# Two-layer hybrid encoder on one core: another rule for the order of the engines' streams, two means placed later, and the first weight's transfer behind x's first square

## The chip, the cores and the metric

The kernel runs on one core of a Trainium2 chip. The metric is the device time of one execution in microseconds (us), the median of several. The engines of the core work beside one another, each through its own list of instructions in order: TensorE (PE, matmuls), VectorE (DVE), ScalarE (ACT), GpSimd (POOL) and SyncE (SP), which here issues most of the transfers (DMAs). Semaphores make an instruction wait for those of other engines on which it depends.

## The reference

The input is x with 512 positions and 1024 channels, and 256 memory tokens. Each of two layers mixes positions by three attention branches, then channels by a gated MLP:

```
mem_n = rms_norm(mem, mem_norm_g)
for l in range(DEPTH):
    h = rms_norm(x, g_pre_mix[l])
    proj = h @ w_in[l]
    # q, k, v of branch A (2-D neighbourhood attention), of branch B
    # (dilated windows), q of branch M (attention into mem_n @ w_mem_kv[l]), gates
    merged = gates_A * (o_a @ w_br_a[l]) + gates_B * (o_b @ w_br_b[l]) + gates_M * (o_m @ w_br_m[l])
    x = x + rms_norm(merged @ w_out[l], g_post_mix[l])
    h = rms_norm(x, g_pre_ffn[l])
    u = depthwise_conv_centred(h @ w_up[l], conv_w[l], conv_b[l])
    a, b = split(u)
    x = x + rms_norm((gelu(a) * b) @ w_down[l], g_post_ffn[l])
```

rms_norm divides by the root of the mean square over the 1024 channels and multiplies by a gain.

## The kernel before

Channels lie on the partitions: x is eight tiles (KD = 8) of 128 channels by 512 positions, worked on in two halves of 256 positions (`HALVES`). Every matmul operand in float32 is split into a high and a low part of the type fp32r, and one product is three matmuls: high by high, high by low, low by high (`mm3`). The high part is a cast on ACT, the low part a subtraction on DVE or POOL (`split`).

Weights come in pieces of 128 columns, 512 KB. `weights` issues the transfer on SP's queue into a buffer `wraw` (three of them), then splits it, into `whi` and `wlo` (two buffers each) or into tiles `m`. SP issues in its own order, and a transfer waits there until its buffer is free; what stands behind it waits too.

A norm is spread over the engines. ACT squares x, DVE adds the squares, PE sums over the partitions with a matmul by the constant column `mean` (`pt<-mean,y` or `pt<-mean,acc`), ACT takes the root, DVE the reciprocal, PE spreads it over the partitions with two transposes (`pt<-ident,st`), and DVE and ACT make the normed and split `h`. `rstd_job` holds these steps; the functions whose names end in `_job` call it. `pre_norm_job` makes h at the start, for each half of x; `mem_norm_job` does it for the memory tokens; `raw_end_job` is the norm of x's second half at the passage from layer 0 to layer 1.

The order of PE's instructions is set in the code: the class `Woven` keeps a clock that each matmul advances by an assumed cost, and jobs are generators that `yield` a delay; when the clock has passed it, their next instructions are put between the matmuls. `spawn` takes a delay, too: `SD1` is that of `pre_norm_job` for x's second half. Every matmul is chained to the one before it, so this order is fixed. The order on DVE, ACT, POOL and SP is chosen by the framework's scheduler (`TileContext`), from the dependences, the code's order and a simulation of when each instruction could run. The start transfers x's first half in four parts, then the weights of the first group (two pieces, then x's second half, then the vectors, then four pieces of which the buffers allow one at once), and the mask and two tables for the attention. Near 60 us PE makes keys and values from the memory tokens in four products (`mm_704`, `mm_745`, `mm_786`, `mm_819`), with the `mm` pool of three PSUM banks; the results are taken out of the bank by halves by a cast on ACT (`m_729`, `m_770`) and a subtraction on DVE (`m_730`, `m_771`).

Of the kernel before, what the change touches and what calls it, by code (L numbers as in the profile page):

```python
# [9 lines left out]
AF = mybir.ActivationFunctionType  # L10
# [15 lines left out]
HALVES = (slice(0, 256), slice(256, 512))  # L26
# [9 lines left out]
LAT_QK, LAT_SM, LAT_T, LAT_V, LAT_T2 = 1.0, 4.5, 1.5, 2.0, 0.6  # L36
STEP_A, STEP_B, STEP_M = 9.0, 9.0, 5.5
SQG, LOG, GEN, KVE = {0: (), 1: ()}, {0: (), 1: ()}, 'GGVGVG', 'VVGG'
SD1 = 4.0
MARGIN = 0.3  # L40
SB = True
TAILG = (0, 2, 4, 6)
# [77 lines left out]
def tile_hybrid_encoder(ctx, tc, xT, memT, memg, vecs, rpb, w_in, w_kv, w_bra, w_brb, w_brm,  # L120
                        w_out, w_up, w_down, c_ident, c_mask, c_tab0, c_tab1, out):
    nc = tc.nc
# [10 lines left out]
    ps_t = ctx.enter_context(tc.tile_pool(name="ps_t", bufs=2, space=bass.MemoryType.PSUM))  # L133
    ps_o = ctx.enter_context(tc.tile_pool(name="ps_o", bufs=1, space=bass.MemoryType.PSUM))

    uid, last_copy, last_act, crit, last_lo = [0], [None], [None], [None], {}
    wv = Woven(tc)

    def nm(s):
        uid[0] += 1  # L140
        return f"{s}_{uid[0]}"
# [8 lines left out]
    def ktile(dt=F32R, shape=(128, 512)):  # L150
        return tp.tile(list(shape), dt, tag="ka", name=nm("ka"), bufs=12)

    def ytile(shape=(128, 512)):
        return tp.tile(list(shape), F32, tag="y", name=nm("y"), bufs=8)
# [23 lines left out]
    ACT, V = Counted(nc.scalar, wv, 0.1, 0.8e-3), Counted(nc.vector, wv, 0.065, 1.05e-3)  # L178
# [10 lines left out]
    def xh(k, half):  # L189
        return xs[:, half.start // 256, k, :]  # L190
# [23 lines left out]
    tab1 = const.tile([128, 2, 256], F32, name="tab1")  # L214


    def behind(ins, other):

        if other is not None and ins is not other:
            tc.add_manual_dep(ins, other.name, ORDER, reason="issue order")  # L220

    def split(src, hi, lo, eng=None):
        last_copy[0] = ACT.copy(hi, src).ins
        last_lo[eng or V] = (eng or V).tensor_sub(lo, src, f32(hi)).ins

    def weights(src, K, C, slot=None, eng=None, after=None):

        raw = wp.tile([128, K, C], F32, tag="wraw", name=nm("wraw"))
        nc.sync.dma_start(out=raw, in_=src)
        if slot is None:  # L230
            hi = wp.tile([128, K, C], F32R, tag="whi", name=nm("whi"), bufs=2)
            lo = wp.tile([128, K, C], F32R, tag="wlo", name=nm("wlo"), bufs=2)
            split(raw, hi, lo, eng)
            behind(last_copy[0], after)
            return [(hi[:, k, :], lo[:, k, :]) for k in range(K)]
        n = 512 // C
        w = []
        for k in range(0, K, n):
            c = min(n, K - k)
            hi, lo = slot(F32R, (128, c, C)), slot(F32R, (128, c, C))  # L240
            split(raw[:, k:k + c, :], hi, lo, eng)
            w += [(hi[:, i, :], lo[:, i, :]) for i in range(c)]
        return w
# [69 lines left out]
    def sumsq_add(acc, src, first, slot=None, eng=None):  # L313
        if first:
            ACT.activation(acc, src, AF.Square)
        else:
            n = acc.shape[-1]
            sq = slot((128, 256)) if slot else small("sq2", 4) if n == 256 else small("sq", 1, (128, 512))
            ACT.activation(sq, src, AF.Square)
            (eng or V).tensor_add(acc, acc, sq)  # L320
# [4 lines left out]
    def rstd_job(accs, n, box):  # L325

        nb = n // 128
        bank = tbank((128, n + nb))
        pr, pt = bank[:, 0:n], bank[:, n:n + nb]
        for i, a in enumerate(accs):  # L330
            for b in range(nb):
                mm(pt[:, b:b + 1], a[:, 128 * b:128 * b + 128], mean, i == 0 and b == 0,
                   i == len(accs) - 1 and b == nb - 1, 0.11)
        rs = smalls(nb)
        crit[0] = ACT.activation(rs, pt, AF.Sqrt, bias=eps, scale=1.0).ins
        V.reciprocal(rs, rs)
        yield 0.8
        for b in range(nb):
            one = rs[:, b:b + 1]
            spread = bass.AP(one.tensor, one.offset, [list(one.ap[0]), [0, 128]])  # L340
            wv.pe(nc.tensor.transpose(pr[:, 128 * b:128 * b + 128], spread, ident), 0.11)
        box.append(pr)

    def normed(src, g, rs, hi, lo, eng=None):
        h32 = small("h32", 3)
        V.scalar_tensor_tensor(out=h32, in0=src, scalar=g, in1=rs, op0=ALU.mult, op1=ALU.mult)
        split(h32, hi, lo, eng)

    def raw_split(l, goff, k, src, hi, lo):

        g = vec[:, l, goff + k:goff + k + 1]
        ACT.activation(hi, src, AF.Copy, scale=g)
        V.scalar_tensor_tensor(out=lo, in0=src, scalar=g, in1=f32(hi), op0=ALU.mult, op1=ALU.subtract)

    def rtile():
        return tp.tile([128, 512], F32, tag="R", name=nm("R"), bufs=1)
# [6 lines left out]
    def pre_norm_job(l, goff, acc, hs, i):  # L363
        half, box = HALVES[i], []
        yield from rstd_job(acc if isinstance(acc, list) else [acc[:, half]], 256, box)
        for k in range(KD):
            g = g0[:, k:k + 1] if l == 0 and goff == V_PRE else vec[:, l, goff + k:goff + k + 1]
            normed(xh(k, half), g, box[0], hs[k][0][:, half], hs[k][1][:, half],
                   G if k in LOG[l > 0 and goff == V_PRE] else V)
        crit[0] = last_copy[0]  # L370
        yield 1.2
        wv.give(f"h{l}.{goff}.{i}")
# [44 lines left out]
    def raw_end_job(l, goff, og, acc, acc2, nxt, lat):  # L417


        half, box = HALVES[1], []  # L420
        hs, raw, R = nxt
        yield lat
        raw.extend((t[:, 0, :], t[:, 1, :]) for t in [ktile(F32R, (128, 2, 256)) for _ in range(KD)])
        yield from rstd_job([acc[:, half]], 256, box)
        for k in range(KD):
            V.tensor_mul(og[k][:, half], og[k][:, half], box[0])
            V.tensor_add(xh(k, half), xh(k, half), og[k][:, half])
            raw_split(l + 1, V_PRE, k, xh(k, half), *raw[k])
            if k == 0:
                yield 0.6  # L430
            wv.give(f"raw{k}")
            yield 1.05
        for k in range(KD):
            sumsq_add(acc2[:, half], xh(k, half), k == 0)
        yield 3.5
        box = []
        yield from rstd_job([acc2[:, half]], 256, box)
        ACT.copy(R[:, half], box[0])
        wv.give("R")
        for k in range(KD):  # L440
            normed(xh(k, half), vec[:, l + 1, V_PRE + k:V_PRE + k + 1], box[0], hs[k][0][:, half], hs[k][1][:, half])
        crit[0] = last_copy[0]
        yield 1.2
        wv.give(f"h{l + 1}.{V_PRE}.1")
# [33 lines left out]
    def mem_kv(l, hm, km, vm, pre=()):  # L478
        wv.need(f"mem{l}")
        for m in range(4):  # L480
            w = pre[m] if pre else weights(w_kv[l, m], KD, 128)
            ps = mmbank((128, N_MEM))
            linear(ps, w, hm, slice(0, N_MEM))
            if m < 2:
                t, u = big(F32R, (128, 2, N_MEM)), big(F32R, (128, 2, N_MEM))
                twice_split(ps, (t[:, 0, :], t[:, 1, :]), (u[:, 0, :], u[:, 1, :]), None, MDUP)
                km.append((t, u))
            else:
                vT = big(F32, (128, 256))
                ACT.copy(vT, ps)  # L490
                wv.spawn(mem_v_job(l, vT, vm))


    def group_weights(srcs, engs):
        return [weights(s, KD, 128, big, e) for s, e in zip(srcs, engs)]
# [19 lines left out]
    def proj(l, m, hs, after=None):  # L515
        w = weights(w_in[l, m], KD, 128, after=after)
        ps = mmbank()
        linear(ps, w, hs)
        return ps
# [344 lines left out]
    def first_squares(half):  # L864
        sqs = [ytile((128, 256)) for _ in range(KD)]
        for k in range(KD):
            ACT.activation(sqs[k], xh(k, half), AF.Square)
            if k % 2:
                V.tensor_add(sqs[k], sqs[k], sqs[k - 1])
            if k in (3, 5) and half != HALVES[0]:  # L870
                V.tensor_add(sqs[k], sqs[k], sqs[k - 2])
        return sqs[1::2] if half == HALVES[0] else sqs[5::2]
# [10 lines left out]
    idle(2)  # L883
    hs = h_tiles()
    wv.spawn(pre_norm_job(0, V_PRE, first_squares(HALVES[0]), hs, 0))
    gw = group_weights([w_in[0, m] for m in FIRST[:2]], (V, V))
    load_x(HALVES[1])
    nc.sync.dma_start(out=vec, in_=vecs)
    wv.need(f"h0.{V_PRE}.0")
    with tc.issue_after(last_copy[0]):  # L890
        sqs = first_squares(HALVES[1])
    wv.spawn(pre_norm_job(0, V_PRE, sqs, hs, 1), SD1)
    gw += group_weights([w_in[0, m] for m in FIRST[2:]], (V, G, V, G))
# [6 lines left out]
    for l in range(depth):  # L900
# [99 lines left out]
        else:  # L1000
            hm, km, vm = [], [], []
            wv.spawn(mem_norm_job(l + 1, hm, htile), 20.0)
            pre, R, raw, box = [], rtile(), [], []
# [119 lines left out]
```

## Time and profile before

| what | value |
|---|---|
| median of 3 runs | 1555.45 us (1555.26 to 1555.7) |
| profiled execution | 1552.91 us |
| its span (first to last instruction) | 1550.9 us |
| mean granted clock of TensorE | 0.995 |
| instructions | 20677 |
| PE, share of the span | 98% |
| weight loads on PE | 84% |
| DVE | 61% |
| ACT | 48% |
| POOL | 10% |
| moved by DMA | 144.91 MB, mean 93 GB/s |

A row of the timeline has the start in us from the start of the span, the duration, the engine, the line of the kernel, the operation, its output and inputs by their names without numbers, and the shapes. "x4" says that four such instructions stand in a row, with the duration from the start of the first to the end of the last. In brackets stands the idle time of the engine ahead of it, and what ended it. L114 is the line of a helper through which ACT's and DVE's operations go, L246 that of the matmuls, L257 and L341 of transposes, L224 of the split, L229 of the weights' transfers. A row of the windows has the window, its length, the busy time and count of an engine, the granted clock (PEclk), the share of the DMA engines and GB/s.

### The profile page before, as it was taken

Reading aid. Unit: us, or ns where it says so; the run is one execution under the profiler, and the core shown is the slowest. Engines: PE = TensorE matmul, PEld = TensorE weight load, DVE = VectorE, ACT = ScalarE, POOL = GpSimd, SP = SyncE. Lnnn points to the kernel's source line nnn. Section 1 sums busy time; section 2 is a strip of 40 time slices with the busy share of each in tenths; the row PEclk is TensorE's granted clock in tenths of the full one; section 3 lists DMA queues with packets and bytes.
Section 4 is the critical chain, followed back from the end, with each engine's and each line's share of the span. In section 5 each row is a group of like instructions: output and inputs, shape, how many; then the busy total and the mean of one; then the engine's idle time right before and its main releaser. Section 6 shows DMA issues by size and latency. Waiting matters only on the chain.

```text
span 1550.9 us, 20677 instructions
## 1 busy us (share of the span) xinstructions
PE 1522.6 (98%) x7970; PEld 1300.1 (84%) x7970; DVE 948.8 (61%) x1684; ACT 739.7 (48%) x1288; POOL 148.6 (10%) x216
## 2 busy tenths in 40 slices
PE   8999999999999999999989999999999999999997
PEld 7988878888988888888888888888889888888887
DVE  6685666335777777743397856753456977776233
ACT  6465575235544444533355556742354544444231
POOL 3340000210000000010154300002100000000000
PEclk9999999999999999999999999999999999999998
DMA  7221113234112332333431221132350223233331
GB/s 246 91 90 61 61 57 98 93 95 157 61 55 96 99 104 96 108 96 102 129 103 59 79 69 58 52 109 88 102 177 15 82 96 98 102 99 89 98 105 62
DMA packets 45810, 144.91 MB, mean 93 GB/s; under 512 B 5376, under 2 KB 9600, under 8 KB 45712
## 3 DMA queue, kind: packets, MB, share of 16 engines
q1 hardware_dynamic: 43776, 139.85, 28.0%
q10 hardware_dynamic: 1296, 2.10, 0.4%
q0 software_dynamic: 640, 1.64, 0.4%
q8 instruction: 62, 1.02, 0.3%
q14 instruction: 36, 0.29, 0.1%
HBM read 141.48 MB, written 2.10 MB: 93 GB/s over the span
## 4 chain that ended last, share of the span: by engine, by line
PE 91%; DVE 5%; ACT 2%; DMA 1%; issue 1%; SPq 0%; ACTq 0%; DVEq 0%
PE mm L246 80%; PE s L246 4%; PE o L246 3%; PE pt L257 2%; DVE y L114 1%; DVE m L114 1%; PE pt L246 1%; DVE x L114 1%; DVE ka L114 1%; DVE acc L114 1%; ACT y L114 0%; DMA vec<-in_vecs_dram 0%; DVE wlo L114 0%; ACT m L114 0%; ACT whi L114 0%
## 5 line engine op out<-in xcount | busy, mean ns | idle before, releaser
L246 PE MATMUL mm<-h,whi 128*128 128x512 f32 x2496 | 775.5, 392 | 0.0
L246 PEld LDWEIGHTS mm<-h,whi 128*128 128x128 f32 x2496 | 461.4, 188 | 90.9
L246 PE MATMUL mm<-h,wlo 128*128 128x512 f32 x1248 | 486.3, 390 | 0.0
L114 DVE TENSOR_TENSOR wlo<-wraw,whi 128x1024 fp32r<-128x1024 f32 (+1 forms) x213 | 259.1, 1217 | 284.2 <-ACT whi L114 281.4
L114 ACT CAST whi<-wraw 128x1024 fp32r<-128x1024 f32 (+1 forms) x213 | 221.1, 1038 | 305.8 <-PE mm L246 292.0
L246 PEld LDWEIGHTS mm<-h,wlo 128*128 128x128 f32 x1248 | 234.3, 188 | 49.6
L246 PE MATMUL mm<-m,whi 128*128 128x512 f32 (+1 forms) x800 | 215.1, 356 | 0.9 <-DVE m L114 0.8
L246 PEld LDWEIGHTS mm<-m,whi 128*128 128x128 f32 x800 | 141.8, 189 | 22.8 <-PE mm L246 1.3
L246 PE MATMUL mm<-m,wlo 128*128 128x512 f32 (+1 forms) x400 | 142.2, 355 | 0.0
L114 DVE SCALAR_TENSOR_TENSOR y<-y,vec,y 128x511 f32<-128x511 f32 x176 | 130.4, 747 | 3.5 <-ACT y L114 0.9
L114 DVE TENSOR_TENSOR y<-mm,R 128x512 f32<-128x512 f32 x82 | 56.3, 687 | 68.4 <-PE mm L246 68.4
L246 PEld LDWEIGHTS mm<-m,wlo 128*128 128x128 f32 x400 | 75.5, 189 | 10.9
L801 POOL TENSOR_TENSOR m<-m,y 128x512 f32<-128x512 f32 x28 | 36.0, 1287 | 402.4 <-DVE y L114 402.4
L114 ACT ACTIVATE y<-y,vec 128x512 f32<-128x512 f32 x88 | 70.9, 813 | 2.1 <-DVE y L114 1.9
L246 PE MATMUL mm<-m,m 128*128 128x512 f32 x240 | 63.6, 395 | 0.0
L114 ACT ACTIVATE y<-y 128x512 f32<-128x512 f32 x44 | 27.8, 632 | 72.3 <-DVE y L114 71.9
L114 DVE TENSOR_TENSOR acc<-acc,sq 128x256 f32<-128x256 f32 (+1 forms) x80 | 41.0, 513 | 27.3 <-ACT sq L114 25.4
L114 ACT CAST m<-pt 128x512 fp32r<-128x512 f32 (+1 forms) x72 | 38.4, 540 | 40.5 <-PE pt L257 31.8
L114 ACT ACTIVATE y<-mm,vec 128x512 f32<-128x512 f32 (+1 forms) x91 | 57.4, 630 | 0.1
L114 DVE TENSOR_TENSOR m<-pt,m 128x512 fp32r<-128x512 f32 (+1 forms) x72 | 44.9, 629 | 18.8 <-ACT m L114 17.9
L114 ACT ACTIVATE y<-y,st 128x256 f32<-128x256 f32 (+1 forms) x80 | 43.7, 547 | 26.7 <-DVE st L114 26.6
L114 ACT CAST m<-y 128x512 fp32r<-128x512 f32 x32 | 19.8, 619 | 72.5 <-DVE y L114 72.5
(152 smaller groups left out, 1808.6 us busy)
## 6 DMA issues: line engine op xcount, KB each, us to landing
wraw<-in_w_in_dram SPq DMA_DIRECT2D x88, 512.0 KB, 3.7
wraw<-in_w_up_dram SPq DMA_DIRECT2D x88, 512.0 KB, 3.6
wraw<-in_w_down_dram SPq DMA_DIRECT2D x32, 512.0 KB, 3.5
wraw<-in_w_out_dram SPq DMA_DIRECT2D x16, 512.0 KB, 4.2
wraw<-in_w_down_dram SPq DMA_DIRECT2D x16, 384.0 KB, 3.1
wraw<-in_w_kv_dram SPq DMA_DIRECT2D x8, 512.0 KB, 4.1
wraw<-in_w_bra_dram SPq DMA_DIRECT2D x16, 192.0 KB, 2.3
x<-in_xT_dram SPq DMA_DIRECT2D x8, 256.0 KB, 5.9
```

Source lines behind the costliest of these rows:

```text
L114: return op(*args, **kw)
L246: wv.pe(nc.tensor.matmul(ps, a, b, start=first, stop=last), cost)
L257: wv.pe(nc.tensor.transpose(ps[:, 128 * i:128 * i + 128], s, ident), 0.11)
L801: (V if br == 2 and m >= 6 else G).tensor_add(acc[m], acc[m], gs)
```

## The change

Four things are changed. The scheduler that orders the engines' streams goes by a timeline simulation (`schedule_with_timeline_sim=True`). `SD1` is 6.0 instead of 4.0, and the delay ahead of the mean in `raw_end_job` 5.0 instead of 3.5. The transfer of the first weight depends on ACT's first square of x (`landed`), so that SP does not issue it, nor what stands behind it, until that square has ended.

```diff
-SD1 = 4.0
+SD1 = 6.0
...
+    first_square = []
...
+    def landed(ins, other):
+        tc.add_manual_dep(ins, other.name, mybir.DependencyInfo(mybir.DependencyClass.Sync, mybir.DependencyReason.DATA),
+                          reason="behind x")
...
         raw = wp.tile([128, K, C], F32, tag="wraw", name=nm("wraw"))
-        nc.sync.dma_start(out=raw, in_=src)
+        load = nc.sync.dma_start(out=raw, in_=src).ins
+        if first_square:
+            landed(load, first_square.pop())
...
         for k in range(KD):
             sumsq_add(acc2[:, half], xh(k, half), k == 0)
-        yield 3.5
+        yield 5.0
         box = []
         yield from rstd_job([acc2[:, half]], 256, box)
...
         for k in range(KD):
-            ACT.activation(sqs[k], xh(k, half), AF.Square)
+            ins = ACT.activation(sqs[k], xh(k, half), AF.Square).ins
+            if k == 0 and half == HALVES[0]:
+                first_square.append(ins)
...
-    with _tile.TileContext(nc) as tc:
+    with _tile.TileContext(nc, schedule_with_timeline_sim=True) as tc:
```

PE's order differs at three places: the mean of x's second half at the start, that of the memory tokens' norm (six matmuls later), and the one of `raw_end_job`. DVE's and ACT's orders differ throughout. On SP, the mask and the two tables now stand ahead of the fifth and sixth pieces of the program, `wraw_250` and `wraw_260`. Numbers behind a name tell buffers of one kind apart; lines are numbered by each kernel's own file.

PE at the start, where the first group's products of x's first half (`h_111` to `h_126`) go into four banks, `mm_283`, `mm_284`, `o_285` and `pt_286`. Before:

```order
L246 MATMUL mm_284<-h_123,m_164 128x256
L246 MATMUL pt_331<-mean,y_223 128x1 x2
L246 MATMUL pt_331<-mean,y_225 128x1 x2
L246 MATMUL mm_283<-h_125,m_153 128x256
L246 MATMUL mm_283<-h_126,m_153 128x256
L246 MATMUL mm_283<-h_125,m_154 128x256
```

Of the change:

```order
L253 MATMUL pt_286<-h_111,m_252 128x256
L253 MATMUL pt_286<-h_112,m_252 128x256
L253 MATMUL pt_286<-h_111,m_253 128x256
L253 MATMUL o_285<-h_113,m_242 128x256
L253 MATMUL o_285<-h_114,m_242 128x256
L253 MATMUL o_285<-h_113,m_243 128x256
L253 MATMUL pt_286<-h_113,m_252 128x256
L253 MATMUL pt_286<-h_114,m_252 128x256
L253 MATMUL pt_286<-h_113,m_253 128x256
L253 MATMUL pt_349<-mean,y_223 128x1 x2
L253 MATMUL pt_349<-mean,y_225 128x1 x2
L253 MATMUL o_285<-h_115,m_242 128x256
```

The mean of x's second half (inputs y_223 and y_225) moved past 18 matmuls: six of mm_283 and mm_284, and twelve of o_285 and pt_286, which need the tiles m_252 and m_253 made from wraw_250.

ACT at the memory tokens' keys and values. Before:

```order
L114 CAST whi_782<-wraw_780 128x1024
L114 CAST m_729<-mm_704 64x256 x2
L114 CAST whi_815<-wraw_813 128x1024
L114 CAST m_770<-mm_745 64x256 x2
L114 CAST whi_914<-wraw_912 128x1024
```

Of the change:

```order
L114 CAST whi_782<-wraw_780 128x1024
L114 CAST m_729<-mm_704 64x256
L114 CAST whi_815<-wraw_813 128x1024
L114 CAST m_770<-mm_745 64x256
L114 CAST m_729<-mm_704 64x256
L114 CAST m_770<-mm_745 64x256
L114 CAST whi_914<-wraw_912 128x1024
```

The second half of m_729, taken from the bank of the first product, moved past the weight cast whi_815 and the first half of m_770. DVE's subtractions moved in the same way: the second half of m_730 behind wlo_816 and the first half of m_771.

PE at the passage to layer 1, where `raw_end_job` places the mean of x's second half between the products of the raw x (`ka_7296` and on). Before:

```order
L246 MATMUL mm_7271<-ka_7296,m_7024 128x256
L246 MATMUL pt_7514<-mean,acc_6079 128x1 x2
L246 MATMUL mm_7270<-ka_7297,m_7001 128x256 x2
L246 MATMUL mm_7270<-ka_7297,m_7002 128x256
L246 MATMUL mm_7271<-ka_7297,m_7023 128x256 x2
```

Of the change:

```order
L253 MATMUL mm_7270<-ka_7298,m_7005 128x256 x2
L253 MATMUL mm_7270<-ka_7298,m_7006 128x256
L253 MATMUL mm_7271<-ka_7298,m_7027 128x256 x2
L253 MATMUL mm_7271<-ka_7298,m_7028 128x256
L253 MATMUL pt_7526<-mean,acc_6079 128x1 x2
L253 MATMUL mm_7270<-ka_7299,m_7005 128x256 x2
```

The mean moved past the twelve matmuls of ka_7297 and ka_7298; the two transposes that spread the factor moved with it.

## The prediction, before the change was run

> **What bounds the kernel.** I read the page's busy table and chain first.
>
> ```profile
> PE 1522.6 (98%) x7970; PEld 1300.1 (84%) x7970; DVE 948.8 (61%) x1684; ACT 739.7 (48%) x1288; POOL 148.6 (10%) x216
> PE 91%; DVE 5%; ACT 2%; DMA 1%; issue 1%; SPq 0%; ACTq 0%; DVEq 0%
> ```
>
> TensorE (PE) is busy for 1522.6 of the 1550.9 us of the span and carries 91% of the chain. The change neither adds nor removes a matmul, so only PE's 28 us of idle time, and stretches at a lower clock, can move the end. PE waits at few places; its list of waits names them (total, count, longest).
>
> ```profile
> PE pt L246 <- DVE acc L114: 4.6, 2, 3.4
> PE pt L257 <- DVE y L114: 3.1, 3, 2.1
> PE pt L246 <- DVE y L114: 2.4, 2, 1.4
> PE s L246 <- DVE st L114: 1.6, 4, 0.5
> ```
>
> All wait for VectorE (DVE), which is busy 61% of the time: its order decides here, and that is what the change alters. The clock comes next: windows with the busy time of PE and the granted clock (PEclk).
>
> ```profile
> 20.76:24.17 3.41, 2.27 (x19) 1.00 0.20 47
> 24.17:27.58 3.41, 3.41 (x18) 0.50 0.73 243
> 781.92:785.34 3.42, 0.37 (x4) 1.00 0.54 165
> 785.34:788.75 3.41, 3.41 (x17) 0.50 0.01 2
> 870.67:874.08 3.41, 1.59 (x8) 1.00 0.20 59
> ```
>
> Two stretches of 3.41 us ran at half clock, each right behind a stretch with a wait; one costs half of 3.41, 1.7 us. A window with 1.59 us of busy PE was not followed by one.
>
> The profiled execution took 1552.91 us, 2.0 us of it outside the span; the median shown is 1555.45, 2.5 above. I make the sum against 1552.91 and carry it to the median.
>
> **The start (held transfer, SD1, x's second half).** Rows of SyncE's queue (SPq), ScalarE (ACT), PE and POOL, and two groups of transfers, those of the first weights in the first 12 us and of the kv weights (count, size, median us to landing).
>
> ```profile
> 0.76 1.81 SPq L195 DMA_DIRECT2D x<-in_xT_dram  x4
> 2.60 0.92 SPq L229 DMA_DIRECT2D wraw<-in_w_in_dram  x2
> wraw<-in_w_in_dram SPq DMA_DIRECT2D x3, 512.0 KB, 6.7
> 3.56 1.48 ACT L114 ACTIVATE y<-x 128x256 f32<-128x256 f32 x4 [0.87 <-DMA x<-in_xT_dram]
> 6.43 1.44 ACT L114 ACTIVATE y<-x 128x256 f32<-128x256 f32 x4 [1.39 <-DMA x<-in_xT_dram]
> 9.57 0.26 ACT L114 ACTIVATE st<-pt,eps 128x2 f32<-128x2 f32 x1 [1.69 <-PE pt L246]
> 11.32 0.40 ACT L114 CAST h<-h 128x256 fp32r<-128x256 f32 x1 [0.47 <-DVE h L114]
> 21.27 1.12 ACT L114 CAST m<-wraw 128x512 fp32r<-128x512 f32 x2
> 21.90 1.05 PE L246 MATMUL pt<-mean,y 128*128 128x1 f32 x8 [1.40 <-DVE y L114]
> 22.47 2.70 POOL L224 TENSOR_TENSOR m<-wraw,m 128x512 fp32r<-128x512 f32 x2 [16.31 <-ACT m L114]
> 36.86 5.20 PE L246 MATMUL mm<-h,m 128*128 128x256 f32 x42
> 38.06 1.98 ACT L114 CAST whi<-wraw 128x1024 fp32r<-128x1024 f32 x2
> wraw<-in_w_kv_dram SPq DMA_DIRECT2D x8, 512.0 KB, 4.1
> ```
>
> The first weight left at 2.60 and shared the queue with x: ACT stood 1.39 us for x's third part. Held until the first square ends (3.56 + 0.4), it leaves 1.4 later, and so does all behind it on SP: the second weight, x's second half, the vectors, the third weight. x may land sooner, by at most those 1.39 us. Between the squares and the first h cast, however, ACT now has all four casts of the first two weights, one ahead of the root (9.57). The second weight landed near 3.09 + 6.7 = 9.8; 1.4 later would put the first h cast near 12.3, 1.0 late, and an unchanged landing 0.8 early. Both ends stay; I take 0.4 early, nearer the latter because x and the weights still share the same queues.
>
> At 21.90 PE waited 1.40 us for the squares' sums of x's second half. The mean now stands 18 matmuls later, so this wait goes. Next late is pt_286<-h_111,m_253: it needs POOL's first subtraction (2.70/2 = 1.35 us), behind a cast that ACT makes behind the eight squares (21.27 + 0.6). POOL starts then near 21.9 and ends near 23.2, while PE, free from 20.5 (21.90 less 1.40), has work for only 11 matmuls of about 0.11 us, until 21.7: a wait of about 1.5 takes the place of the old one. I count nothing for the pair, and keep the half clock behind it. **Start: -0.4; bounds +1.0 and -3.5 (wait and half-clock stretch both gone).**
>
> For x's second half, ACT now makes the two kv weight casts (38.06 before) and four squares of memory ahead of the first h cast. The casts need weights whose buffers come free by POOL's pair (25.2) and DVE's subtractions (some 1.5 later); with 4.1 us to landing that is 29.3 and near 31. With the h casts behind them I get the first h near 33.2 and the last near 41.0, PE's use of the last being near 41.9. That covers it by 0.9 us: nothing in the sum, but each further microsecond late costs one.
>
> SP issues the mask and two tables ahead of two weights. Those weights wait for buffers, so I cost it at nothing; the room of 0.9 us is what hides an error.
>
> **Memory K and V near 60 us.** Rows of ACT, DVE and PE.
>
> ```profile
> 60.59 0.37 ACT L114 CAST m<-mm 64x256 fp32r<-64x256 f32 x1 [1.47 <-DVE m L114]
> 60.98 1.05 ACT L114 CAST whi<-wraw 128x1024 fp32r<-128x1024 f32 x1
> 60.99 0.43 DVE L114 TENSOR_TENSOR m<-mm,m 64x256 fp32r<-64x256 f32 x1 [0.43 <-ACT m L114]
> 62.06 1.23 DVE L114 TENSOR_TENSOR wlo<-wraw,whi 128x1024 fp32r<-128x1024 f32 x1 [0.64 <-ACT whi L114]
> 61.56 0.47 PE L246 MATMUL mm<-m,whi 128*128 128x256 f32 x2 [0.84 <-DVE m L114]
> ```
>
> PE starts the third product at 61.56, once the second half of m_730 has left the first product's bank. Before, the cast m_729 (0.37) stood ahead of whi_815 (1.05); now whi_815 and half of m_770 stand ahead of it, and on DVE wlo_816 (1.23) and half of m_771 (0.42) ahead of m_730. whi_815 needs the buffer that PE reads until it stops, about 60.6 (61.56 less 0.84 is 60.7). So: cast 60.6 to 61.65, wlo_816 to 62.9, m_771 to 63.3, m_730 to 63.75, PE near 63.9. **+2.3**; bounds +1.0 (if the buffer comes free early, so that wlo_816 is nearly done by 61.5 and little more than the two halves of m_771 and m_770, 0.42 and 0.37, is added) and +4.0 (with a half-clock stretch of 1.7).
>
> The Trainium skill's page "TensorE: Matmul & The Clock Gate", Part 1: The HAM clock gate, says that the clock halves after at least one idle window of about 3.4 us in a free-running grid; by it a wait of 3.2 us would never cost that, and the upper end would be +2.3. The trace agrees on the length of 3.41, but not on idleness: the window 20.76 to 24.17 had 2.27 us of busy PE and was still followed by half clock.
>
> **The end of layer 0 near 781 us.**
>
> ```profile
> 771.81 2.21 DVE L114 TENSOR_TENSOR x<-x,y 128x256 f32<-128x256 f32 x2
> 777.82 0.41 DVE L114 TENSOR_TENSOR x<-x,y 128x256 f32<-128x256 f32 x1
> 778.00 4.24 POOL L224 TENSOR_TENSOR m<-wraw,m 128x512 fp32r<-128x512 f32 x3 [1.39 <-ACT m L114]
> 784.97 0.64 PE L246 MATMUL pt<-mean,acc 128*128 128x1 f32 x4 [3.44 <-DVE acc L114]
> ```
>
> PE's longest wait, 3.44 us, is for the sums of squares of x's first half. DVE's additions from SBUF take 0.41 alone but up to 1.5 while POOL subtracts. The new order first makes all eight multiplications by the PSUM factor, then eight additions to x, then the sums. The additions still pass at about one per POOL subtraction; two casts now ahead of the squares hold ACT until their weight lands near 773.7, but let POOL go on sooner. Following the rows in the new order I get the last sum between 784.4 and 785.8, against 784.8. **+0.3**, bounds -1 and +2; the half clock behind it stays.
>
> The Trainium skill's page "SBUF — State Buffer", section SBUF: two separate sides, makes this an exclusive lock: a DVE operation with two SBUF inputs and a GpSimd operation that reads SBUF wait for one another in full. By it the eight additions would cost at least the rest of four to five subtractions, the later of my two ends (+1). The 0.41 beside 1.5 us agrees.
>
> **The end of x's second half near 813 us.**
>
> ```profile
> 811.39 2.29 PE L246 MATMUL mm<-ka,m 128*128 128x256 f32 x18
> 814.83 0.58 PE L246 MATMUL pt<-mean,acc 128*128 128x1 f32 x4 [1.16 <-DVE acc L114]
> ```
>
> The mean moves 12 matmuls later, 12 x 0.12 = 1.44 us (2.29/18 is 0.127, with the end of the last in it), more than the wait of 1.16 and some 0.15 of refilling. The factor comes later by as much; I found no PE row that waits for it now, so that costs nothing. **-1.3**, bounds -1.3 and 0 (if DVE's sums end 1.4 later).
>
> **Small waits that DVE's and ACT's order moves.**
>
> ```profile
> 172.02 0.69 DVE L114 SCALAR_TENSOR_TENSOR ka<-mm,ka 64x512 fp32r<-64x512 f32 x1
> 173.24 0.71 PE L246 MATMUL s<-m,m 128*128 128x128 f32 x4 [0.45 <-DVE st L114]
> 195.25 0.56 DVE L114 TENSOR_TENSOR m<-wraw,m 128x384 fp32r<-128x384 f32 x1
> 244.54 1.05 ACT L114 CAST whi<-wraw 128x1024 fp32r<-128x1024 f32 x1
> 248.07 0.59 PE L257 MATMUL pt<-ident,y 128*128 128x128 f32 x2 [0.51 <-DVE y L114]
> ```
>
> Near 172, and at the same step of layer 1, the score reduction now stands ahead of the 0.69 us operation: 0.6 saved twice, -1.2 (the 0.45 and the refilling of PE). Near 194 a weight subtraction of 0.56 now stands ahead of the reduction that PE waits for: about +0.25, twice, +0.5. Near 247 the weight cast of 1.05, with its subtraction, moves some 6 us ahead, out of the path to the transpose: -0.5 of the 0.51 and its refilling, twice, -1.0. Other exchanges at value matmuls delay by about 0.4 what has 0.4 to 1.0 of room: 0 to +1, taken +0.4. Together **-1.3**, bounds -3 and +1.5.
>
> **Sum:** -0.4 + 2.3 + 0.3 - 1.3 - 1.3 = -0.4. 1552.91 becomes 1552.5, and the median 1555.1.
>
> **Rivals.** *Faster:* the start keeps its clock. If PE's new wait is shorter than I think, the 1.4 and the 1.7 both go: -3.1 on my -0.4 gives -3.5, and with the short waits at their better end -5.2: 1550.3. For it speaks that 1.59 us of busy PE sufficed once; against it that POOL's subtraction cannot start before 21.8 and PE has no other work.
>
> *Slower:* ACT works in order, and casts moved ahead hold it while their weight or buffer is missing. Its place is x's second half: if the second kv weight lands over 0.9 us later than I get (after about 31.5), the last h misses its use. At 4 us late (3.1 beyond) with the half clock near 62 (1.7), -0.4 + 3.1 + 1.7 = +4.4: 1559.9. For it speaks that four weights follow one another through three buffers there; against it that the tables now move before.
>
> *It does not do what it says:* the weights land later by what x lands sooner, and the four casts ahead of the first h take it back. Then the start is worth 0 to +1 and the sum is 0 to +1: inside the forecast.
>
> **How the numbers follow.** About 0.2% (3.1 us) is what a measurement of this kernel can tell from no change. The forecast, with the third rival in it, has 0.46 and its own range is 1552.4 to 1558.5; faster has 0.30, more than one row speaks for, since many small terms lean that way; slower 0.24. To hold 8 in 10 the range runs from 1549.0, past the faster case, to 1560.5, past the slower one; one in ten is left at each side. Predicted 1555.1.
>
> **What would show it.** Right: PE idle near 60.7 for about 3.2 us, waiting for DVE m; a wait of about 1.5 for POOL near 21.7; no wait near 813; about 3.4 to 4 us still near 781. Wrong: full clock between 20 and 28 us, PE waiting for h near 41, third kv product near 61.6 as before, or waits at places where PE has none now.

## The result, and the profile after

The change made the kernel slower: median 1569.85 us (1568.66 to 1572.16, 4 runs) against 1555.36 us, a ratio of 1.0096 with a 95% interval of 1.0080 to 1.0113. The prediction was 1555.1 in a range of 1549.0 to 1560.5: the time lies 9 us above the range. The profiled execution took 1571.04 us, 18.1 more than the one before. One execution, of the experiment e2 below, ran at a clock of 0.80 and took 2813 us; it is left out of the ratios.

The page of the change, its busy row, then the chain:

```profile
PE 1527.6 (97%) x7970; PEld 1300.1 (83%) x7970; DVE 952.0 (61%) x1684; ACT 737.5 (47%) x1288; POOL 149.7 (10%) x216
PE 86%; DVE 6%; DMA 3%; ACT 3%; issue 1%; POOL 0%; SPq 0%; DVEq 0%; ACTq 0%
```

PE makes the same 7970 matmuls, but 5 of its 91% of the chain have gone to DVE, ACT and DMA. Its waits (total, count, longest):

```profile
PE pt L264 <- DVE y L114: 4.9, 6, 1.6
PE pt L348 <- DVE st L114: 4.4, 4, 2.2
PE pt L253 <- DVE acc L114: 4.0, 1, 4.0
PE mm L253 <- DVE m L114: 3.2, 1, 3.2
PE mm L253 <- DVE h L114: 2.7, 3, 1.1
PE mm L253 <- ACT h L114: 2.3, 2, 1.9
PE mm L253 <- DVE wlo L114: 2.3, 4, 0.8
...
PE pt L253 <- POOL m L229: 0.9, 1, 0.9
...
PE pt L253 <- ACT m L114: 0.2, 1, 0.2
```

One wait for acc is left of two: that near 813 is gone here (in a second trace of the change, e14, 0.85 us of it is back). Against it stand more and longer waits for y, st and wlo, a wait for m of 3.2 instead of 0.8, and more waits for h. Since both kernels run the same matmuls, and almost everywhere in the same order, the start of one and the same matmul in both traces shows where the time went. The table gives by how much the change's lag behind the kernel before grew in each stretch (times of before):

| stretch, us | lag grows by, us | the prediction's term |
|---|---|---|
| 0 to 34, the start | -0.9 | -0.4 |
| 34 to 46, h of x's second half | +5.6 | 0, "covers it by 0.9 us" |
| 46 to 66, memory K and V | +3.5 (wait 2.3, half clock 1.2) | +2.3, bound +4.0 |
| 66 to 764, many places | +5.4 | a part of -1.3 |
| 764 to 790, the end of layer 0 | +0.6 | +0.3 |
| 790 to 820, the end of x's second half | -1.3 | -1.3 |
| 820 to the end, many places | +5.0 | a part of -1.3 |

Where h is late, DVE, SP's queue, the transfer issued at 26.01 (size, us to landing), ACT, DVE and PE of the change show this, and the last line the first h cast of the kernel before:

```profile
23.41 2.58 DVE L114 TENSOR_TENSOR m<-wraw,m 128x512 fp32r<-128x512 f32 x2 [0.79 <-ACT m L114]
26.01 0.64 SPq L234 DMA_DIRECT2D wraw<-in_w_kv_dram  x1
wraw<-in_w_kv_dram SPq DMA_DIRECT2D x1, 512.0 KB, 7.8
29.20 1.05 ACT L114 CAST whi<-wraw 128x1024 fp32r<-128x1024 f32 x1 [3.21 <-DMA wraw<-in_w_kv_dram]
33.88 1.05 ACT L114 CAST whi<-wraw 128x1024 fp32r<-128x1024 f32 x1 [3.62 <-DMA wraw<-in_w_kv_dram]
36.07 0.70 ACT L114 CAST h<-h 128x256 fp32r<-128x256 f32 x2
31.43 0.87 DVE L114 SCALAR_TENSOR_TENSOR h<-x,g,pt 128x256 f32<-128x256 f32 x2
39.05 0.86 DVE L114 SCALAR_TENSOR_TENSOR h<-x,g,pt 128x256 f32<-128x256 f32 x2
44.48 0.86 DVE L114 SCALAR_TENSOR_TENSOR h<-x,g,pt 128x256 f32<-128x256 f32 x2
37.97 5.02 PE L253 MATMUL mm<-h,m 128*128 128x256 f32 x24 [1.07 <-DVE h L114]
43.94 3.30 PE L253 MATMUL mm<-h,m 128*128 128x256 f32 x21 [0.94 <-DVE h L114]
25.62 0.41 ACT L114 CAST h<-h 128x256 fp32r<-128x256 f32 x1 [0.82 <-DVE h L114]
```

The second kv weight is issued at 26.01, when DVE's two subtractions have ended (23.41 + 2.58 = 25.99), and lands 7.8 us later, near 33.85. ACT stands 3.21 and 3.62 us for the two kv weights, whose casts are ahead of the first h cast in its order; that comes at 36.07 instead of 25.62. DVE makes two normed tiles from 31.43 on and the others later, the last two from 44.48 on, and PE follows at that pace. In this execution the stretch 38.76 to 42.17 also ran at half clock; e14 kept the full clock there and still lost 5.0 us between 34 and 46, so the wait for h carries the loss.

At the memory's K and V, ACT, DVE and PE of the change, then windows (length, busy PE, clock) here and at other places:

```profile
65.33 1.04 ACT L114 CAST whi<-wraw 128x1024 fp32r<-128x1024 f32 x1 [1.57 <-PE mm L253]
66.28 0.75 ACT L114 CAST m<-mm 64x256 fp32r<-64x256 f32 x2
66.41 1.22 DVE L114 TENSOR_TENSOR wlo<-wraw,whi 128x1024 fp32r<-128x1024 f32 x1 [1.32 <-ACT whi L114]
67.55 1.27 DVE L114 TENSOR_TENSOR m<-mm,m 64x256 fp32r<-64x256 f32 x3
68.56 0.48 PE L253 MATMUL mm<-m,whi 128*128 128x256 f32 x2 [3.15 <-DVE m L114]
```

```profile
24.17:27.58 3.41, 3.41 (x32) 1.00 0.33 91
35.35:38.76 3.41, 1.91 (x14) 1.00 0.73 272
38.76:42.17 3.41, 3.36 (x15) 0.50 0.19 56
66.07:69.48 3.41, 0.92 (x8) 1.00 0.56 189
69.48:72.89 3.41, 3.41 (x19) 0.50 0.39 136
885.27:888.68 3.41, 2.10 (x10) 1.00 0.18 71
```

whi_815 waits 1.57 us for its buffer, all else follows, and PE's wait is 3.15 as worked out. The clock then fell to a half from 69.48 to 72.89. At the start, by contrast, the stretch 24.17 to 27.58, at half clock in the kernel before, kept the full clock in this execution.

Two of the many small places. First DVE and PE near 431, where before PE did not wait for the reciprocal; then ACT and PE near 670.

```profile
428.74 1.41 DVE L114 TENSOR_TENSOR y<-y,pt 128x256 f32<-128x256 f32 x4
430.06 2.44 DVE L114 TENSOR_TENSOR x<-x,y 128x256 f32<-128x256 f32 x7
432.41 0.17 DVE L114 RECIPROCAL st<-st 128x2 f32<-128x2 f32 x1
432.63 0.43 PE L348 MATMUL pt<-ident,st 128*128 128x128 f32 x2 [0.83 <-DVE st L114]
662.83 0.42 ACT L114 ACTIVATE h<-h 128x256 f32<-128x256 f32 x1 [1.77 <-DMA h<-in_memT_dram]
666.15 0.42 ACT L114 ACTIVATE sq<-h 128x256 f32<-128x256 f32 x1 [1.56 <-DMA h<-in_memT_dram]
666.47 0.62 ACT L114 ACTIVATE y<-y 128x512 f32<-128x512 f32 x1
667.09 1.28 ACT L114 ACT_TABLE_LOAD   x1
669.11 1.03 ACT L114 CAST whi<-wraw 128x1024 fp32r<-128x1024 f32 x1
671.72 0.50 PE L253 MATMUL mm<-m,wlo 128*128 128x512 f32 x1 [0.78 <-DVE wlo L114]
```

The same places in the kernel before:

```profile
420.39 0.17 DVE L114 RECIPROCAL st<-st 128x2 f32<-128x2 f32 x1 [0.31 <-ACT st L114]
421.43 0.38 PE L341 MATMUL pt<-ident,st 128*128 128x128 f32 x2
654.57 1.03 ACT L114 CAST whi<-wraw 128x1024 fp32r<-128x1024 f32 x1
655.50 0.41 ACT L114 ACTIVATE h<-h 128x256 f32<-128x256 f32 x1
```

Near 431 DVE makes the last four of eight multiplications and seven additions in a row, and the reciprocal of 0.17 us that PE needs stands behind them. Before, it was ready 0.87 us ahead of PE (420.56 against 421.43). Near 670 squares of the memory tokens for layer 1, for whose transfers ACT waits 1.77 and 1.56 us, now stand ahead of an activation, a table load and the weight cast; before, the cast came first.

### The profile page after: what moved, and what is told of

It is laid out like the page before. It is cut to its first block, busy times and chain, and to the rows that moved or that the text cites. A ratio compares the mean times of both kernels' runs of the same rounds, so it can differ in the third digit from the quotient of the medians.

```text
span 1569.2 us, 20667 instructions
## 1 busy us (share of the span) xinstructions
PE 1527.6 (97%) x7970; PEld 1300.1 (83%) x7970; DVE 952.0 (61%) x1684; ACT 737.5 (47%) x1288; POOL 149.7 (10%) x216
## 4 chain that ended last, share of the span: by engine, by line
PE 86%; DVE 6%; DMA 3%; ACT 3%; issue 1%; POOL 0%; SPq 0%; DVEq 0%; ACTq 0%
PE mm L253 77%; PE s L253 4%; PE o L253 3%; PE pt L264 2%; DVE y L114 1%; DVE m L114 1%; DVE h L114 1%; PE pt L253 1%; DMA wraw<-in_w_in_dram 1%; ACT whi L114 1%; DVE x L114 1%; DMA wraw<-in_w_kv_dram 1%; DVE wlo L114 1%; DMA wraw<-in_w_down_dram 1%; DMA x<-in_xT_dram 1%
## 5 line engine op out<-in xcount | busy, mean ns | idle before, releaser
L253 PE MATMUL mm<-h,m 128*128 128x256 f32 x312 | 50.9, 308 | 5.2 <-DVE h L114 2.7
L114 DVE TENSOR_TENSOR m<-wraw,m 128x512 fp32r<-128x512 f32 (+1 forms) x58 | 39.2, 690 | 25.9 <-ACT m L114 25.7
```

What stands on the lines that cost most here:

```text
L114: return op(*args, **kw)
L253: wv.pe(nc.tensor.matmul(ps, a, b, start=first, stop=last), cost)
```

## The experiments

**The four parts, taken apart.** First the order alone (e1):

```diff
-    with _tile.TileContext(nc) as tc:
+    with _tile.TileContext(nc, schedule_with_timeline_sim=True) as tc:
```

> The kernel before with the timeline-simulation order alone; no held transfer, SD1 4.0, delay 3.5. If the new order of ACT and DVE is the cause (theory A): +13 to +17 us against before, with PE waiting for h between 36 and 47 us (4 to 6 us), for m near the third kv product (about 3.2) and the many small waits. If the held transfer (B) makes the weights of 30 us late: at most +9, no wait for h at 36 to 47. If the later means (C) do: no wait for h, under +5.

It took 1566.51 us against 1554.36, ratio 1.0079 (1.0062 to 1.0096): +12.2. Theory A holds for most of the loss, but not in its place: PE did not wait for h between 36 and 47 here: the lag behind the kernel before was -0.7 near 27 us, -0.9 from 28 to 61, and grew again only at the third kv product. The wait for h needs something else.

The change without that line (e2):

> The change without the timeline simulation: held transfer, SD1 6.0, delay 5.0, streams ordered as before. Theory A: -3 to +1 us against before, the kv wait at 0.8 as before, no wait for the mean near 813. Theories B and C: +5 or more, from PE waiting for h of x's second half.

It took 1558.22 us, ratio 1.0025 (1.0015 to 1.0034): +3.9, so neither theory's figure. The parts left over cost something even in the old order. The parts alone, priced below, add to +4.5 (7.2 - 2.7 + 0.0).

The change without the held transfer (e3):

```diff
-            landed(load, first_square.pop())
+            first_square.pop()
```

> The change without the held transfer, with every engine's order as in the change. Theory A: within 2 us of the change (1568 to 1571), wait for h at 36 to 47 still 4 to 6 us. Theory B: 5 or more faster than the change, because the second kv weight lands before 32 instead of 33.9.

1571.04 us, ratio 1.0102 (1.0084 to 1.0120), and its waits for h are still there:

```profile
PE mm L253 <- DVE h L114: 2.5, 3, 1.6
```

The second kv weight's cast started at 33.21, against 33.88 in the change, and not before 32. The hold is not the cause; B falls.

The change with both delays as before (e4):

```diff
-SD1 = 6.0
+SD1 = 4.0
...
-        yield 5.0
+        yield 3.5
```

> The change with SD1 4.0 and the delay 3.5, timeline simulation and held transfer kept. Theory A: within 3 us of the change, above it by the wait near 813 (1.3) and the start's mean. Theory C: 5 or more faster than the change, since the transposes of x's second half come 1.5 us earlier and so do its h tiles.

1566.52 us, ratio 1.0078 (1.0063 to 1.0093), the same as the order alone and 3.3 below the change, with no wait for h between 36 and 47. Neither theory has the size: A wanted it above the change and within 3 us, C at least 5 below. The wait for h goes with the old delays, as C says, and the wait near 813 is back.

**Which of the means, and why.** Reading the orders again showed what SD1 6.0 does: the job of the memory norm has the delay 6.0 too. With 4.0 the h tiles of x's second half are issued ahead of the memory norm; with 6.0 only their mean is, and the memory's squares, its running sum (in one of the three buffers `h32` that the h tiles also pass through) and the kv weights come ahead of them in the program. So SD1 6.0 alone (e5):

```diff
-SD1 = 4.0
+SD1 = 6.0
```

> The kernel before with SD1 6.0 alone. Theory A1 (with 6.0 the memory norm, whose delay is also 6.0, comes ahead of the h tiles of x's second half in the program, takes one of the three h32 buffers and has its squares and kv weights served first): +3 to +6 us, PE waiting for h between 36 and 47. Rival A2 (that wait needs the timeline order): within 1 us of before, or 1 to 2 faster because the wait at 21.9 goes.

1561.95 us, ratio 1.0048 (1.0031 to 1.0065): +7.2 in the old order. Its list of waits of PE has this line, where the kernel before has a single wait of 0.9:

```profile
PE mm L246 <- DVE h L114: 2.6, 3, 1.4
```

By the same matmuls, its trace loses 2.9 us between 34 and 46. Another 2.7 are lost ahead of 34, where the half clock lasted 6.8 instead of 3.4 us and PE waited for ACT and POOL, and 1.4 at a half-clock stretch near 880. So the wait for h is not the whole of the 7.2. Here no kv cast stands ahead of the first h cast, which still comes at 36.13, behind squares of memory tokens that landed from 33.3 on.

The delay in `raw_end_job` alone (e6):

```diff
         for k in range(KD):
             sumsq_add(acc2[:, half], xh(k, half), k == 0)
-        yield 3.5
+        yield 5.0
```

> The kernel before with the delay 5.0 in raw_end_job alone. By the prediction's term: -1.3 us, no wait of PE for acc near 813. Rival: the factor's later arrival is felt behind it and the time is 0 to +1.

1552.03 us, ratio 0.9982 (0.9973 to 0.9991). The wait near 813 is gone and the lag falls by 1.4 there; the -2.7 of the medians is more (the interval reaches from -1.4 to -4.2).

SD1 6.0 with the memory norm behind it (e7):

```diff
-    wv.spawn(mem_norm_job(0, hm, big), 6.0)
+    wv.spawn(mem_norm_job(0, hm, big), 8.0)
```

> The kernel before with SD1 6.0 and the delay of the memory norm 8.0 instead of 6.0, so that x's second half stays ahead of the memory tokens in the program. Theory A1: no wait for h between 36 and 47, time within 2 us of before (a wait of up to 1.5 may appear at the first product of K and V, whose operands come 2 us later). Rival A3 (the later mean itself is what makes h late): +3 to +6 as with SD1 6.0 alone.

1556.58 us, ratio 1.0007 (0.9998 to 1.0017); no wait for h between 36 and 47, and none at the first product of K and V. For the wait for h the mean's place does not matter by itself; that the memory norm came first does. A3 falls. The later mean is not free, though: this trace loses 1.6 us ahead of 34, and the median is 1.9 above the kernel before.

The held transfer alone, that is the change with SD1 4.0, the delay 3.5 and without the timeline order (e8):

> The kernel before with the held first transfer alone. By the prediction's start term: 0 within 1 us (x's third part lands sooner, the weights later). If the hold is what helps: -1 to -3. If the later weights decide: +1 to +2, first matmul of the projection near 12.8 instead of 11.8.

1554.76 us, ratio 0.9998 (0.9988 to 1.0007): nothing, inside what the start's term had. Its first matmul of the projection came 0.9 earlier than in the kernel before, but so did that of the run with the delay 5.0 alone, which holds nothing; the hold can't be told from chance there.

**Inside the timeline order.** Two order edges put the cast whi_815 and wlo_816 behind the first product's evacuation (the edges order instructions on one engine and wait for nothing else; e9):

```diff
+            if m == 3 and not pre:
+                behind(last_copy[0], first[0])
+                behind(last_lo[V], first[1])
...
+                if m == 0:
+                    first = (last_copy[0], last_lo[V])
```

> The timeline order alone, with two order edges that put the cast whi_815 and the subtraction wlo_816 behind the two halves of the first product's m_729 and m_730. Theory (the order at that place costs 2 to 4 us): PE's wait for m falls from about 2.5 to about 1.7, the half-clock stretch behind it goes, -1.5 to -3 against the timeline order alone (1566.5), so 1563.5 to 1565. Rival (something else holds m_730): no change.

1564.08 us, ratio 1.0062 (1.0039 to 1.0086). PE's wait there:

```profile
61.52 0.47 PE L246 MATMUL mm<-m,whi 128*128 128x256 f32 x2 [1.46 <-DVE m L114]
```

The wait fell from 3.2 to 1.46 and full clock followed; compared by the same matmuls, the kernel is 2.8 to 3.1 us ahead of the order alone from there on.

An edge from each addition to x to the next multiplication, at the ends of the sublayers (e10):

```diff
-            V.tensor_mul(og[k][:, half], og[k][:, half], box[0])
-            V.tensor_add(xh(k, half), xh(k, half), og[k][:, half])
+            behind(V.tensor_mul(og[k][:, half], og[k][:, half], box[0]).ins, summed)
+            summed = V.tensor_add(xh(k, half), xh(k, half), og[k][:, half]).ins
```

> The timeline order alone, with an order edge from each addition to x to the next multiplication by the factor at the ends of the sublayers (not at the output), so that DVE does not run all eight multiplications first. Theory (that order makes the reciprocals near 421 and 1186 late, 1.25 us each, and the sums near 785 by 0.7): -2.5 to -4 against the timeline order alone, 1562.5 to 1564. Rival (the wait comes from ACT's order): within 1 us of 1566.5.

1565.80 us, ratio 1.0069 (1.0046 to 1.0092): within 1 us of the order alone in the median, so the sum missed. The places did move: near 421 and 1186, where the order alone loses 1.0 each, the lag no longer grows, and the transposes near 426 start without a wait. This speaks for DVE's order as the cause there, against the rival. But the scheduler, given other edges, made other choices, and near 660 and 800 the kernel lost 1.2 and 0.9 more than the order alone.

**The change once more, with the memory norm later (e12).**

> The whole change with the memory norm's delay 8.0 instead of 6.0. Theory A1: the wait for h between 36 and 47 goes (5 us), 1564 to 1567, against 1570 of the change. Rival (the timeline order makes that wait by itself when the mean is late): 1568 to 1571.

1569.68 us, ratio 1.0094 (1.0074 to 1.0114). The wait for h was gone, yet the time was that of the rival. To settle what SD1 costs in the change, three kernels were timed on one chip: the change with SD1 4.0 (e13),

> The whole change with SD1 4.0. If SD1 costs in the change what it costs alone (7 us), 1563 to 1565; if it costs nothing there (as the change with the memory norm at 8.0 might say), 1568 to 1571. No wait for h between 36 and 47 in either case.

the change (e14),

> The change as it is, on the same chip as its two variants, so that the three can be told apart to 1 us: 1568 to 1572.

and the change with the memory norm at 8.0 (e15).

> The change with the memory norm's delay 8.0, again, beside the other two. If only the clock hid the gain of the vanished wait for h, 1565 to 1568; if the gain is given back by waits that come with the later memory norm, 1568 to 1571.

They took 1565.64, 1571.48 and 1568.16 us (ratios 1.0071, 1.0101, 1.0079). SD1 costs 5.8 in the change. The third has 3.3 of that gain, between the two cases expected; its six times lie between 1563.42 and 1569.45. Its profiled execution, by windows of PE (length, busy, clock), and then the same windows of the change beside it:

```profile
20.47:23.88 3.41, 1.78 (x12) 1.00 0.06 25
23.88:27.30 3.42, 3.42 (x19) 0.50 0.36 119
27.30:30.71 3.41, 3.41 (x18) 0.50 0.82 243
36.00:47.00 11.00, 11.00 (x95) 1.00 0.23 85
```

```profile
20.47:23.88 3.41, 2.44 (x19) 1.00 0.30 111
23.88:27.30 3.42, 3.11 (x26) 1.00 0.17 40
36.00:47.00 11.00, 7.90 (x52) 1.00 0.25 90
```

PE is busy for 11.00 instead of 7.90 us of the stretch 36 to 47, but ran 6.8 us before it at half clock, 3.4 us lost, which the change did not. By the same matmuls it is 2.4 us later than the change at 34 and 2.6 ahead at 50: in this execution the slower start hid about half of the gain. That the two fastest runs (1563.42 and 1564.85) are those without it is only likely: their mean clocks are 0.993 and 0.992, those of the others 0.989 to 0.991, but they have no profile.

**What is left when only the good parts are kept:** the delay 5.0 and the held transfer, with SD1 4.0 and the old order (e11).

> The kernel before with the delay 5.0 and the held transfer, without the timeline order and with SD1 4.0: the two parts that did not cost. If they add: 1551 to 1553, 1.5 to 3 faster than before.

1551.96 us, ratio 0.9980 (0.9970 to 0.9989), 2.4 faster than before: faster than both kernels, and no better than the delay alone.

## Why the prediction was wrong

The parts alone give +12.2 (order), +7.2 (SD1), -2.7 (delay) and 0.0 (hold), +16.7 together; the change has +14.5. With intervals of 2.6 us to either side on the first two, the difference of 2.2 is not told from nothing.

- **The step that failed first: "That covers it by 0.9 us: nothing in the sum".** I had seen that the kv casts stood ahead of the h casts, and had priced it as the slower rival, but gave it nothing in the sum. The second kv weight did not land "near 31". Its buffer came free even sooner than I had reckoned (25.99, not 26.7), but I had given the transfer the median of 4.1, and it took 7.8 (7.2 in e14), with the memory tokens' transfers, issued from 25.74 on, under way beside it. ACT then reached the first h cast at 36.07, not 33.2. A weight late by 2.9 was worth 2.0 by the slower rival's price; the stretch lost 5.6. The rest came because the h tiles did not follow without a break, as I had them: the last casts began at 44.98, not near 41.0. One of the three h32 buffers belonging to the memory's sum fits that; it was not tried by itself. I also put the cause in the scheduler's order, while it lay in SD1: with 6.0 the memory norm comes first in the program, under either order.
- **Small waits, "together -1.3": measured about +10.** This is the largest error. The moves that I had picked did what they should in part: -0.6 and -0.7 near 172 and 937. Near 195 and 960 it was +0.35 each instead of +0.25, and near 204 and 969, which I had not listed, +0.5 each. Near 247 and 1011 I expected -0.5 each and it was +0.8: the weight cast did move ahead, but at its new place it stands before a table load and the exponentials, and on DVE a reciprocal that waits 1.08 us for them and a subtraction now stand ahead of the row maximum. What I took at +0.4 for all "other exchanges" holds +1.0 each near 421 and 1186, +1.1 near 850, +1.4 near 831, +1.8 near 658 and +0.6 near 762. I had looked at the places where PE already waited. Nearly all of the loss came where PE had not waited before, and where I had not worked out how long it would stay so; near 421 the room was 0.87. The order alone (e1) loses the same near 247, 421, 850, 1011 and 1186, so there it is the new order; near 658 and 831 it loses only 0.6 and 0.0, and which part makes up the rest was not tried.
- **Memory K and V, +2.3: right**, with the wait of 3.15 for the 3.2 forecast. The half clock behind it, my bound of +4.0, came as well; e9 shows that the order there is the cause.
- **The end of layer 0, +0.3: +0.6**, inside its bounds. **The end of x's second half, -1.3: -1.3** in this trace, and e6 alone has -1.4. In e14, where 0.85 of the wait is back, the stretch gives only -0.4.
- **The start, -0.4: -0.9, the size by luck.** The wait of 1.40 went, and the new waits for ACT and POOL (0.2 + 0.9) came where the prediction put them, shorter than its 1.5. But the first matmul was 1.1 later, by its pessimistic end, and the half clock that I had kept did not come: 1.7 us that the faster rival had, and that hid the late first matmul. e8 prices the hold at nothing.
- **The clock.** The Trainium skill's page "TensorE: Matmul & The Clock Gate", Part 1: The HAM clock gate, asks for an idle window of about 3.4 us. The window ahead of the half clock at 781.92 in the kernel before, with 0.37 us of busy PE, comes near that; those with 0.92 (66.07 to 69.48 here) and 1.78 (e15) do not, and they led to half clock as well.
- **The chances.** 0.24 for slower was too little. An order that differs throughout on DVE and ACT under a PE that is 98% busy can gain at most the 28 us of idle time, the start and the end of the kernel among them, and can lose at every place.

## What to carry to other kernels

When one engine is nearly always busy, check a reordering not only at its waits but at the places where an operand is ready only just in time: here waits appeared where there had been none. Before a delay is changed, look for another job with the same or a near delay: passing it changes who is served first, in buffers and queues as well. Land a transfer with the others that are under way in mind, not by the median of its kind: the kv weight with a median of 4.1 took 7.8 here, 6.2 in e5 and, with the memory norm later in the change, 4.3 in e12. How much each neighbour costs was not tried.

## What the runs showed of the hardware

Within the kernel, the half-clock stretches of the traces read here lasted 3.41 us or a multiple of it. What brings them on was not to be read from the busy time ahead: 1.59 us of busy PE in a window of 3.41 did not (before, 870.67), 2.27 did (before, 20.76), 2.10 did not and 1.91 did (the change, 885.27 and 35.35), 1.78 did (e15), twice in a row. One such stretch costs 1.7 us where PE is busy throughout, which is one source of the spread of one and the same kernel: 1551.36 to 1558.42 for the kernel before in one session. A gain of 2 us in a kernel like this one is told by the start of the same matmul in two traces, place by place and with the clock beside it, sooner than by a few timed runs; the end alone is not enough, for the trace of the hold alone ends 3.7 us behind that of the kernel before, with equal medians.
